# Undivided exponentials, value products with queries on partitions, and head pairs transposed on TensorE in a hybrid attention layer

## The chip, the cores and the metric

The kernel runs on one core of one Trainium2 chip. The metric is the device time of one execution in microseconds (us), lower is better. A core has five engines that run their own instruction streams in order: TensorE (PE, matrix products; PEld are its weight loads), VectorE (DVE), ScalarE (ACT), GpSimd (POOL) and SyncE (SP), which here issues all the transfers. Engines wait for one another by semaphores. Everything is computed in float32, with products split into a high and a low part of lower precision.

## The reference, cut to what matters

One encoder layer on x of 1024 tokens by 1024 channels. Eight latent heads attend to all earlier chunks of 64 tokens; eight chunked heads attend to a band of nine chunks with a position bias. The heads' outputs are laid side by side and multiplied by w_out; a gated MLP follows, which the change does not touch.

```python
def mla_attention(q, k, v):          # per block of 128 queries
    s = einsum('bqhd,bkhd->bhqk', qi, k) * scale
    s = where(mask, s, NEG_INF)
    p = softmax(s, axis=-1)
    return einsum('bhqk,bkhd->bqhd', p, v)

def chunk_attention(q, k, v, rel_bias):   # per chunk of 64 queries, 576 keys
    s = einsum('bqhd,bkhd->bhqk', qch, kb) * scale + bias
    s = where(valid, s, NEG_INF)
    p = softmax(s, axis=-1)
    return einsum('bhqk,bkhd->bqhd', p, vb)
...
mixed = dot(concatenate([o_mla, o_ca], -1), w_out)
x = x + g_a * mixed
```

Both heads have a value width of 64. The mask of the latent heads, in tiles of 128 queries, gives query tile i the keys of tiles 0 to i; a chunked head's tile i takes tiles i-4 to i.

## The kernel before, in words

The program is built by Tile: the Python code traces instructions, pools of named buffers ("tags", each with a number of bufs) give them memory, and a scheduler puts them in an order per engine by priorities and by a timeline of its own, so the order on an engine is not that of the code. A new tile of a tag waits until a buffer of that tag is free.

Attention is cut into units of four query tiles of one head (class Unit). `units` lists first the chunked units c{pair}{odd}, by pair of heads, half g of the sequence and odd or even head, then the latent units m{group}{head}, each head with g = 0 and g = 1 one behind the other. For each tile, `scores` (L634) makes the products q·k in PSUM (tag S, two buffers), the row minimum on DVE (L667 to L675), the exponential on ACT with the sum of the row in rsum (L681), the reciprocal of the sum on DVE (L683, L684), and then, in pieces of at most 640 keys, the divided exponentials as a half-precision high part on POOL (`scale_pool`, L71 from L698) and the rest as a low part on DVE (L701). Both parts lie in one tile of tag HL (three buffers), which a transposing DMA turns into tile PT (L703, three buffers). Exponentials of up to 640 keys lie in tag P (three buffers), longer ones in tag pg (six buffers), which also holds pages of the projections.

`values` (L707) runs three tiles behind `scores` (DEPTH). It multiplies the values with the transposed parts: the stationary operand is the stack of V's high and low part (64 + 64 columns), the moving one the 128 queries, so PSUM tile pv (one buffer, four query tiles side by side) has the head's channels on partitions, V's high part on one half and its low part on the other. After the fourth tile ACT scales one half into sb (L721), DVE adds the other (L722), and the 64 by 512 result goes to DRAM tile oT_d (L723), which holds all heads with channels on partitions.

`qk_page` (L612) makes the pages of q and k of a unit: four transposes on PE into PSUM tag T (one buffer), then a high part on ACT and a low part on DVE, in SBUF tags Q (two) and K (three).

Fillers are products that `pace` draws between the tiles: projections f_v, f_qk, f_m, the latent up-projections f_up (many small operations on POOL), and last f_oca, the output projection of the chunked heads. f_oca (L596) reads oT_d per tile of 128 tokens into `cl`, splits it on ACT (`ch`, L75) and POOL (`cl`, L82), multiplies by w_out and keeps the result in part_d. f_ada loads pieces of w_ada in between. Behind the attention, the loop at L855 does the same for the latent heads (ol, oh), adds part_d, makes the gated residual and the second norm (xn), and transposes it for the MLP (ht_ps).

Row tiles (rtile, tag R, four buffers) and square tiles (qtile, tag sq, two) are of equal size.

Of the kernel before, what the change touches and what calls it, by code (L numbers as in the profile page):

```python
# [41 lines left out]
MODE_C = "1111"  # L42
MODE_M = "1111"
# [3 lines left out]
# columns of the packed constants  # L47
# [15 lines left out]
def layer_kernel(ctx, tc, I, out):  # L63
# [3 lines left out]
    def f32(ap):  # L67
        return ap.bitcast(F32)
# [17 lines left out]
    oT_d = dram.tile([ND, P, S], F32, name="oT_d")  # L86
# [3 lines left out]
    # ---------------- constants  # L90
# [53 lines left out]
    def gemm3(pt, pairs, start=True, stop=True):  # L144
        """pairs: (stationary_hi, stationary_lo, moving_hi, moving_lo)"""
        n = len(pairs)
        for i, (sh, sl, mh, ml) in enumerate(pairs):
            pe.matmul(pt, sh, mh, start=(start and i == 0), stop=False)  # L148
            pe.matmul(pt, sh, ml, start=False, stop=False)  # L149
            pe.matmul(pt, sl, mh, start=False, stop=(stop and i == n - 1))  # L150
# [16 lines left out]
    # ---- weights of one column block of the input projection, split once  # L167
# [23 lines left out]
    # ---- x: statistics and normalised rows  # L191
# [42 lines left out]
    for d in range(ND):  # L234
# [10 lines left out]
        # modT rows: 0 = gain of the norm * (1 + scale), 1 = shift  # L245
# [13 lines left out]
    # ---- rotary tables  # L259
    def rope_tables():  # L260
# [56 lines left out]
        # per token: [g1 cos | g2 cos | g1 sin | g2 sin]  # L317
# [13 lines left out]
    # ---- exact power-of-two scales that bring V into half precision's range, from a bound on |V|:  # L331
    # |sum_d x_d w_d|^2 <= n * sum_d b_d^2 w_d^2
# [83 lines left out]
    # ---- the other adaLN rows  # L416
# [32 lines left out]
    def gate_bcast(pt, acc, c0, w, alloc):  # L449
        """column sums of acc, and b_ada, on every partition"""  # L450
# [53 lines left out]
    # ---- q_up / kv_up of 4 heads: token-layout q, k (normalised, rotated) and V stacks  # L504
# [78 lines left out]
    # ---- output projection of the chunked heads, kept aside in DRAM  # L583
# [11 lines left out]

    def f_oca():  # L596
        for n in range(2):
            ws = load_wo(4, n, "a", "p")
            for t in range(NT):
                lo = rtile(f"cl{t}_{n}", (P, 4, P), F32R)  # L600
                hi = rtile(f"ch{t}_{n}", (P, 4, P), F32R)
                sp.dma_start(f32(lo[:]), oT_d[4:8, :, t * P:(t + 1) * P].rearrange("k p t -> p k t"))
                hi_of("a", hi[:], f32(lo[:]))
                lo_of("p", lo[:], f32(lo[:]), hi[:])
                pt = ps.tile([P, 512], F32, name=f"oc{t}_{n}", tag="mm", bufs=2)
                yield from gemm3_f(pt[:], [(hi[:, k], lo[:, k], ws[k][:, 0], ws[k][:, 1]) for k in range(4)])
                o = qtile(f"co{t}_{n}")
                act.activation(o[:], pt[:], AF.Copy)
                sp.dma_start(part_d[t][:, n * 512:(n + 1) * 512], o[:])
# [16 lines left out]
    class Unit:  # L626
        """4 query tiles of one head"""

        def __init__(u, nm, base, rows, pages, vst, g, band, bias, odd, dst_d, vs):
            u.nm, u.base, u.rows, u.pages, u.vst, u.g = nm, base, rows, pages, vst, g  # L630
            u.band, u.bias, u.odd, u.dst_d, u.vs = band, bias, odd, dst_d, vs
            u.pt = {}

        def scores(u, i):  # L634
            """scores of one query tile and their softmax, transposed in two half-precision parts"""
# [5 lines left out]
            rsum = cst.tile([P, 1], F32, name=f"rs{nm}", tag="rsum", bufs=4)  # L641
            ri = cst.tile([P, 1], F32, name=f"ri{nm}", tag="ri", bufs=4)
            with tc.high_priority(offset=OFF_S):
# [37 lines left out]
                act.activation(pr[:, :n], sv, AF.Exp, bias=m[:], scale=-1.0, accum_out=rsum[:, 0:1])  # L681
            with tc.high_priority(offset=OFF_P):
                dve.reciprocal(ri[:], rsum[:, 0:1])  # L683
                dve.tensor_scalar(ri[:], ri[:], PSCALE, None, op0=MUL)  # L684
                u.pt[i] = []
                for x, (p0, p1) in enumerate(pieces):
# [3 lines left out]
                    cnt[0] += 1  # L690
                    mode = (MODE_C if u.band else MODE_M)[cnt[0] % 4]
                    if mode == "2":
                        scale_pool(pp, pp, ri[:])
                        act.activation(hl[:, :w], pp, AF.Copy)
# [342 lines left out]
```

## Time and profile before

| | us |
|---|---|
| median of three runs | 1521.95 (1520.9, 1521.95, 1524.99) |
| span of the profiled execution | 1526.0 |
| PE busy | 1338.1 (88%) |
| DVE busy | 824.4 (54%) |
| POOL busy | 664.7 (44%) |
| ACT busy | 487.4 (32%) |
| DMA queue of SP, share of 16 engines | 36.0% |
| mean granted clock of PE | 0.928 |

Busy time is an average over stages with different limits, so it is read stage by stage, by windows of the trace. A waiting instruction holds up what stands behind it on its engine. In rows of the trace, `out<-in` are names of tiles; "idle before" is the time that the engine waited ahead of the instruction and what released it. Names end in m for latent heads and in c for chunked ones (Pm, hlm, PTm, sm, pvm); L numbers are lines of the kernel before.

### The profile page before, as it was taken

The page shows a single profiled execution, that of the slowest core. Times are in us where ns is not written, and L with a number is a line of the kernel's source. Part 1 is how long each engine was busy: PE and PEld are TensorE (multiplying, and loading weights), DVE is VectorE, ACT ScalarE, POOL GpSimd, SP SyncE. Part 2 cuts the span into 40 slices and gives each one's busy share as a digit, 9 for nine tenths or more (in the row PEclk, how much of TensorE's full clock was granted, in tenths as well). Part 3 has the DMA queues.
Part 4 walks back from the last instruction along what each step waited for, and adds up shares of the span by engine and source line. Part 5 has one row for each costly group of instructions (what it writes and reads, how often), then busy time and mean ns, then how long its engine had stood idle before and what let it go on. Part 6 is the DMA issues. An engine that isn't in the chain of part 4 may idle for free.

```text
span 1526.0 us, 19445 instructions
## 1 busy us (share of the span) xinstructions
PE 1338.1 (88%) x7100; PEld 1111.0 (73%) x7100; DVE 824.4 (54%) x1536; ACT 487.4 (32%) x919; POOL 664.7 (44%) x720
## 2 busy tenths in 40 slices
PE   3859989998767888858739999999999999999997
PEld 2749878987646666646528888888888888888885
DVE  6864786566768768843742433344334343434343
ACT  5443353343545545532413211212122121221200
POOL 5264463473799735435725231514314142341510
PEclk9979978989878899977859999999999999999998
DMA  7323657463613678787142110202112020110202
GB/s 270 133 67 73 138 119 142 121 131 94 122 40 70 150 143 174 165 181 247 56 138 69 56 55 28 70 30 67 42 42 69 15 83 28 56 56 28 70 1 110
DMA packets 202460, 142.90 MB, mean 94 GB/s; under 512 B 146294, under 2 KB 181242, under 8 KB 201340
## 3 DMA queue, kind: packets, MB, share of 16 engines
q1 hardware_dynamic: 202364, 141.66, 36.0%
q8 instruction: 56, 0.92, 0.3%
q14 instruction: 40, 0.33, 0.1%
HBM read 93.90 MB, written 13.11 MB: 70 GB/s over the span
## 4 chain that ended last, share of the span: by engine, by line
PE 63%; DMA 14%; DVE 10%; POOL 7%; issue 3%; ACT 2%; SPq 1%; POOLq 0%; DVEq 0%; ACTq 0%
PE up L148 10%; PE up L149 10%; PE up L150 10%; DMA aw<-w_ada 6%; PE dn L148 5%; PE dn L149 5%; PE dn L150 5%; DMA PTm<-hlm 4%; PE sc L656 2%; DVE adacc L241 2%; DVE aacc L428 1%; PE sm L656 1%; PE pvc L714 1%; POOL hlm L71 1%; DMA adaw<-w_ada 1%
## 5 line engine op out<-in xcount | busy, mean ns | idle before, releaser
L148 PE MATMUL up<-hT,wu_h 128*128 128x512 f32 x704 | 275.1, 391 | 0.0
L149 PE MATMUL up<-hT,wu_h 128*128 128x512 f32 x704 | 274.3, 390 | 0.0
L150 PE MATMUL up<-hT,wu_l 128*128 128x512 f32 x704 | 274.1, 389 | 0.0
L951 DVE TENSOR_TENSOR x<-x,dn 128x1024 f32<-128x1024 f32 x88 | 107.4, 1220 | 179.8 <-PE dn L150 179.8
L924 DVE SCALAR_TENSOR_TENSOR u<-up,pk,u 128x1023 f32<-128x1023 f32 x44 | 56.4, 1283 | 232.1 <-ACT u L923 232.1
L923 ACT ACTIVATE u<-up,pk 128x1024 f32<-128x1024 f32 x44 | 53.1, 1208 | 386.0 <-PE up L150 386.0
L149 PEld LDWEIGHTS up<-hT,wu_h 128*128 128x128 f32 x704 | 132.4, 188 | 28.0 <-issue 0.5
L148 PEld LDWEIGHTS up<-hT,wu_h 128*128 128x128 f32 x704 | 132.4, 188 | 27.9 <-issue 0.5
L82 POOL TENSOR_TENSOR wu_l<-wu_r,wu_h 128x1024 fp32r<-128x1024 f32 x44 | 105.7, 2402 | 107.9 <-PE up L149 60.1
L150 PEld LDWEIGHTS up<-hT,wu_l 128*128 128x128 f32 x704 | 132.4, 188 | 27.7 <-POOL wu_l L82 0.2
L77 POOL TENSOR_SCALAR wd<-wd_r 128x1024 fp32r<-128x1024 f32 x22 | 23.1, 1050 | 290.2 <-PE dn L150 289.1
L148 PE MATMUL dn<-wd,g 128*128 128x512 f32 x352 | 138.0, 392 | 5.0 <-ACT g L75 5.0
L149 PE MATMUL dn<-wd,g 128*128 128x512 f32 x352 | 137.9, 392 | 0.0
L150 PE MATMUL dn<-wd,g 128*128 128x512 f32 x352 | 137.4, 391 | 0.0
L71 POOL TENSOR_SCALAR hlm<-Pm,rim 128x512 f16<-128x512 f32 (+4 forms) x88 | 62.8, 717 | 69.1 <-DMA PTm<-hlm 46.6
L75 ACT ACTIVATE wu_h<-wu_r 128x1024 fp32r<-128x1024 f32 x44 | 46.5, 1057 | 141.1 <-DMA wu_r<-w_up 141.1
L938 POOL TENSOR_TENSOR wd_r<-wd_r,gmbc 128x1024 f32<-128x1024 f32 x22 | 52.6, 2392 | 80.6 <-DMA wd_r<-w_down 80.6
L701 DVE SCALAR_TENSOR_TENSOR hlm<-Pm,rim,hlm 128x512 f16<-128x512 f32 (+4 forms) x88 | 70.2, 801 | 31.7 <-POOL hlm L71 31.4
L148 PEld LDWEIGHTS dn<-wd,g 128*128 128x128 f32 x352 | 66.6, 189 | 19.4 <-issue 5.4
L71 POOL TENSOR_SCALAR hlc<-Pc,ric 128x640 f16<-128x640 f32 (+2 forms) x64 | 45.9, 719 | 78.5 <-DVE ric L684 38.9
L656 PE MATMUL sm<-mk,mq 96*128 96x512 f32 (+3 forms) x288 | 70.0, 375 | 9.8 <-ACT Pm L681 9.0
L656 PE MATMUL sc<-k,q 64*128 64x512 f32 (+3 forms) x288 | 71.2, 376 | 7.4 <-ACT Pc L681 4.9
(276 smaller groups left out, 3031.8 us busy)
## 6 DMA issues: line engine op xcount, KB each, us to landing
wu_r<-w_up SPq DMA_DIRECT2D x44, 512.0 KB, 3.6
aw<-w_ada SPq DMA_DIRECT2D x96, 128.0 KB, 2.2
wd_r<-w_down SPq DMA_DIRECT2D x22, 512.0 KB, 3.5
x<-x SPq DMA_DIRECT2D x16, 512.0 KB, 9.3
adaw<-w_ada_a SPq DMA_DIRECT2D x8, 1024.0 KB, 4.8
wq_r<-w_qk SPq DMA_DIRECT2D x32, 128.0 KB, 2.6
wor<-w_out SPq DMA_DIRECT2D x16, 256.0 KB, 3.0
cl<-oT_d SPq DMA_DIRECT2D x16, 256.0 KB, 3.3
```

The costliest lines, as they stand in the source:

```text
L71: pool.tensor_scalar(o, i, s, 1.0, op0=MUL, op1=MUL)
L75: act.activation(o, i, AF.Copy)
L82: (pool if eng == "p" else dve).tensor_tensor(o, i, f32(hi), op=SUB)
L148: pe.matmul(pt, sh, mh, start=(start and i == 0), stop=False)
L149: pe.matmul(pt, sh, ml, start=False, stop=False)
L150: pe.matmul(pt, sl, mh, start=False, stop=(stop and i == n - 1))
L656: last = pe.matmul(s[:, c:c + w], qpg[rs_, a, q], kpgs[kh][rs_, b, ko:ko + w], start=(a == 0 and b == 0), stop=(a == 1))
L701: dve.scalar_tensor_tensor(hl[:, w:2 * w], pp, ri[:], hl[:, :w], op0=MUL, op1=SUB)
L923: act.activation(u[:], pt[:], AF.Identity, scale=pk[:, cv + 2:cv + 3], bias=pk[:, cv + 3:cv + 4])
L924: dve.scalar_tensor_tensor(u[:, 1:], pt[:, :S - 1], pk[:, cv + 1:cv + 2], u[:, 1:], op0=MUL, op1=ADD)
L938: pool.tensor_tensor(raw[:], raw[:], gmbc[:], op=MUL)
L951: dve.tensor_tensor(x1[t][:], x1[t][:], pt[:], op=ADD)
```

## The change

- Exponentials are split undivided: the high and low part are made with the constant PSCALE in place of PSCALE over the sum of the row. The sums of a unit's four tiles are kept in one tile of 128 by 4.
- The value product swaps its operands: the transposed exponentials are stationary, the stack of V moves, so that pv has queries on partitions and, for each query tile, 64 columns of V's high part and 64 of its low part.
- After four tiles, ACT copies one half, DVE adds the other, and POOL multiplies by the reciprocals of the sums. Both heads of a pair write into one tile of 128 queries by 4 tiles by 128 channels.
- After the odd head, qk_page transposes that tile on PE through PSUM tag T into a page of tag K, with high and low part made there, and the page (512 KB) goes to DRAM; oT_d is now a separate tile per pair and half.
- f_oca and the loop behind the attention load these pages instead of splitting on ACT and POOL. f_oca holds four pages of tag pg for a half of the sequence and all eight weight tiles of both column halves; its loops are exchanged.
- Tags R (four) and sq (two) become one tag R of five; tag sb goes, and tag o has three buffers for one; rsum and ri change from four buffers of one column to three of four columns.
- Modes that were not in use, and comments, are gone.

```diff
-    oT_d = dram.tile([ND, P, S], F32, name="oT_d")
+    oT_d = [[dram.tile([P, 2, 512], F32, name=f"oT_d{k}_{h}") for h in range(2)] for k in range(ND)]
...
-        return apg.tile(list(shape), dt, name=name, tag="R", bufs=4)
+        return apg.tile(list(shape), dt, name=name, tag="R", bufs=5)
...
-        return apg.tile([P, 512], F32, name=name, tag="sq", bufs=2)
+        return apg.tile([P, 512], F32, name=name, tag="R", bufs=5)
...
+    def load_oT(k, h, name):
+        pg = pgtile([P, 2, 512], F32R, name)
+        sp.dma_start(f32(pg[:]), oT_d[k][h][:])
+        return pg
+
     def f_oca():
-        for n in range(2):
-            ws = load_wo(4, n, "a", "p")
-            for t in range(NT):
-                lo = rtile(f"cl{t}_{n}", (P, 4, P), F32R)
-                hi = rtile(f"ch{t}_{n}", (P, 4, P), F32R)
-                sp.dma_start(f32(lo[:]), oT_d[4:8, :, t * P:(t + 1) * P].rearrange("k p t -> p k t"))
-                hi_of("a", hi[:], f32(lo[:]))
-                lo_of("p", lo[:], f32(lo[:]), hi[:])
...
+        ws = [load_wo(4, n, "a", "p") for n in range(2)]
+        for h in range(2):
+            pgs = [load_oT(4 + k, h, f"ocl{k}_{h}") for k in range(4)]
+            for j in range(4):
+                sl = slice(j * P, (j + 1) * P)
+                for n in range(2):
+                    pt = ps.tile([P, 512], F32, name=f"oc{h}{j}_{n}", tag="mm", bufs=2)
+                    yield from gemm3_f(pt[:], [(pgs[k][:, 0, sl], pgs[k][:, 1, sl], ws[n][k][:, 0], ws[n][k][:, 1])
+                                               for k in range(4)])
...
-                dve.reciprocal(ri[:], rsum[:, 0:1])
-                dve.tensor_scalar(ri[:], ri[:], PSCALE, None, op0=MUL)
...
-                            scale_pool(hl[:, :w], pp, ri[:])
-                        dve.scalar_tensor_tensor(hl[:, w:2 * w], pp, ri[:], hl[:, :w], op0=MUL, op1=SUB)
+                    scale_pool(hl[:, :w], pp, PSCALE)
+                    dve.scalar_tensor_tensor(hl[:, w:2 * w], pp, PSCALE, hl[:, :w], op0=MUL, op1=SUB)
...
-                    last = pe.matmul(u.pv[:, c], u.vst(j), mov, start=(x == 0), stop=(x == len(todo) - 1))
+                    last = pe.matmul(u.pv[:, c], p, u.vst(j), start=(x == 0), stop=(x == len(todo) - 1))
...
-                    act.activation(sb[r0], u.pv[r1], AF.Copy, scale=inv[r1])
-                    dve.scalar_tensor_tensor(dst[r0], u.pv[r0], inv[r0], sb[r0], op0=MUL, op1=ADD)
-                    sp.dma_start(u.dst_d[r0, u.g * 512:(u.g + 1) * 512], dst[r0])
+                    if not u.odd:
+                        opair[u.pair, u.g] = at.tile([P, 4, 2, 64], F32, name=f"o{u.nm}_{u.g}", tag="o", bufs=3)
+                    o = opair[u.pair, u.g]
+                    ri = cst.tile([P, 4], F32, name=f"ri{u.nm}_{u.g}", tag="ri", bufs=3)
+                    dve.reciprocal(ri[:], u.rsum[:])
+                    pv = u.pv[:].rearrange("p (t a b) -> p t a b", t=4, a=2)
+                    act.activation(o[:, :, u.odd], pv[:, :, 1], AF.Copy)
+                    dve.tensor_tensor(o[:, :, u.odd], o[:, :, u.odd], pv[:, :, 0], op=ADD)
+                    pool.tensor_tensor(o[:, :, u.odd], o[:, :, u.odd], ri[:].unsqueeze(2).to_broadcast([P, 4, 64]), op=MUL)
+            if i % 4 == 3 and u.odd:
+                pg = qk_page(lambda j: o[:, j].rearrange("p a b -> p (a b)"), f"oT{u.nm}_{u.g}", P, "K", 3, vscale[u.vs][1])
+                sp.dma_start(u.dst_d[u.g][:], f32(pg[:]))
...
     for t in range(NT):
-        lo = gb.tile([P, 4, P], F32R, name=f"ol{t}", tag="ol", bufs=3)
-        hi = gb.tile([P, 4, P], F32R, name=f"oh{t}", tag="oh", bufs=3)
-        sp.dma_start(f32(lo[:]), oT_d[0:4, :, t * P:(t + 1) * P].rearrange("k p t -> p k t"))
-        hi_of("a", hi[:], f32(lo[:]))
-        lo_of("p", lo[:], f32(lo[:]), hi[:])
+        if t % 4 == 0:
+            oTs = []
+            for k in range(4):
+                pg = gb.tile([P, 2, 512], F32R, name=f"ol{k}_{t}", tag="ol", bufs=4)
+                sp.dma_start(f32(pg[:]), oT_d[k][t // 4][:])
+                oTs.append(pg)
```

More of the change, by code (lines that the diff above doesn't have):

```diff
@@ L626, in layer_kernel, with __init__ @@
     class Unit:
-        def __init__(u, nm, base, rows, pages, vst, g, band, bias, odd, dst_d, vs):
+        def __init__(u, nm, base, rows, pages, vst, g, band, bias, odd, dst_d, vs, pair):
             u.nm, u.base, u.rows, u.pages, u.vst, u.g = nm, base, rows, pages, vst, g
-            u.band, u.bias, u.odd, u.dst_d, u.vs = band, bias, odd, dst_d, vs
+            u.band, u.bias, u.odd, u.dst_d, u.vs, u.pair = band, bias, odd, dst_d, vs, pair
             u.pt = {}
@@ L640, in scores @@
             nm = f"{u.nm}_{i}"
[L641 to L642 removed]
+            if i % 4 == 0:
+                u.rsum = cst.tile([P, 4], F32, name=f"rs{nm}", tag="rsum", bufs=3)
             with tc.high_priority(offset=OFF_S):
@@ L866, in layer_kernel @@
             gemm3(pt[:, n * 512:(n + 1) * 512],
-                  [(hi[:, k], lo[:, k], wo[n][k][:, 0], wo[n][k][:, 1]) for k in range(4)])
+                  [(oTs[k][:, 0, sl], oTs[k][:, 1, sl], wo[n][k][:, 0], wo[n][k][:, 1]) for k in range(4)])
         dve.tensor_tensor(pa[:], pa[:], pt[:], op=ADD)
```

35 lines of the change are left out of this document (9 added, 26 removed).

## The prediction

> **What bounds the kernel now.** First the busy time by stretch. The stretches are cut where the trace changes work: 97 is the first product of f_v, 517 comes just after the last POOL step of f_up (L580, 515.2 us), 682 after the last value product (L714, 681.0 us), 794 at the first product of the MLP.
>
> ```profile
> core 0: us, PE busy (x) PEld busy (x) DVE busy (x) ACT busy (x) POOL busy (x), PEclk, DMA share, GB/s
> 97.00:400.00 303.00, 284.70 (x1999) 250.28 (x2000) 191.89 (x568) 123.98 (x334) 147.66 (x224) 0.91 0.54 117
> 400.00:517.00 117.00, 86.01 (x468) 68.61 (x467) 90.51 (x235) 63.68 (x154) 109.21 (x195) 0.81 0.35 77
> 517.00:682.00 165.00, 130.33 (x917) 103.17 (x914) 117.97 (x277) 77.00 (x159) 76.96 (x89) 0.93 0.78 163
> 682.00:794.00 112.00, 65.92 (x261) 50.18 (x261) 60.73 (x59) 30.69 (x47) 55.01 (x46) 0.71 0.46 152
> 794.00:1526.00 732.00, 722.09 (x3169) 596.59 (x3167) 287.48 (x220) 144.09 (x133) 231.59 (x110) 0.99 0.17 52
> ```
>
> The MLP (732 us) is PE alone, and the change leaves it as it is. Chunked heads and projections (303 us) have PE busy 94%. Up-projections beside the first latent heads (117 us) have POOL busy 93%. The latent heads (165 us) are full nowhere: PE 79%, DMA 78%, DVE 71%. The output projection (112 us) has no engine above 59%: a chain of waits. For the latent heads, the waits:
>
> ```profile
> POOL hlm L71 <- DMA PTm<-hlm: 46.6, 27, 3.7
> ...
> PE pvm L714 <- DMA PTm<-hlm: 17.5, 17, 2.4
> ```
>
> A piece (up to 640 keys of one query tile) is written by POOL into one of three hl buffers, completed by DVE, and transposed by DMA; POOL waits for a free hl 27 times in 67 pieces. These 67 pieces take 165 us, 2.46 us each. One turn of an hl buffer, 0.69 (POOL) + 0.74 (DVE) + 1.24 (issue) + 3.3 (median landing), about 6.0 us, over three buffers would allow 2.0 us. The rest is DVE's order; its groups here:
>
> ```profile
> L701 DVE SCALAR_TENSOR_TENSOR hlm<-Pm,rim,hlm 128x512 f16<-128x512 f32 x31 | 28.1, 908 | 16.7 <-POOL hlm L71 16.6
> ...
> L722 DVE SCALAR_TENSOR_TENSOR om<-pvm,vabm,sbm 64x512 f32<-64x512 f32 x12 | 8.9, 738 | 2.9 <-ACT sbm L721 2.7
> ...
> L683 DVE RECIPROCAL rim<-rsm 128x1 f32<-128x1 f32 x46 | 7.0, 153 | 5.0 <-ACT Pm L681 4.8
> L684 DVE TENSOR_SCALAR rim<-rim 128x1 f32<-128x1 f32 x46 | 6.8, 148 | 0.7
> ```
>
> **The change, part by part.** *Chunked heads (97 to 400).* Seven of the eight pages of head pairs fall here, each four transposes. Nearest row, over the whole attention:
>
> ```profile
> L82 POOL TENSOR_TENSOR cl<-cl,ch 128x512 fp32r<-128x512 f32 x16 | 20.7, 1293 | 10.7 <-ACT ch L75 9.0 <-PE pvm L714 1.8
> ...
> L616 PE MATMUL k_ps<-ident,qn 128*128 128x128 f32 x32 | 5.1, 276 | 0.5 <-DVE q L620 0.5
> ```
>
> 5.1/32 = 0.16 us, so 28 cost 4.5 us on the engine that is 94% busy. Against it stand PE's waits here for transposed pieces (8.5 us) and for exponentials (4.9), which a shorter softmax shortens. Bounds +4.5 and -5; I take +3. The swapped value products keep count and shape (128x128, f16, 219 ns median), so nothing; swapped operands are not in the trace, and I allow 10% of their 0.06 us spacing (about 1056 of them, 6 us) either way, hidden on latent heads.
>
> *Up-projections (400 to 517).* In the built order of POOL, 21 pieces precede the last step of f_up before the change, 13 after it. The cause is in the code: oca's four pages take four of the six pg buffers, which the six latT pages had held and from which score tiles over 640 keys (P of tiles 5, 6, 7) also come. Eight pieces (384, 512, 640 keys, then 512, 256, 512, 384, 512) leave POOL: 0.58 + 5 rows of 0.5 to 0.76 + 1.03 and so on, 5.9 us. One cl (1.29) and one weight residue (1.4) leave; two multiplies of om enter. No row has these (128x256, f32, broadcast): between 0.47 (a 128x256 on DVE) and 1.06 (POOL's 128x512 broadcast L371), I take 0.74, POOL's 128x256 L82. POOL is the bound, so 117 becomes 117 - 5.9 - 1.3 - 1.4 + 1.5 = 110: **-7**.
>
> *Latent heads (517 to 682).* The eight pieces arrive here: 75 x 2.46 = 184.7, **+20**. DVE loses the reciprocal and scale of each tile (7.0 + 6.8 = 13.8) and L722 (8.9); it gains 13 reciprocals of 128x4 (0.15) and 13 adds of 128x256 (0.47, as L409), 8.1, and seven pages at 0.74 (k, L623), 5.2: -9.4. L701 at 512 keys means 908 ns here and is 0.75 in the timeline where POOL has no two-input operation: over all 67 pieces 12.7 us of stretch, beside 23 such operations (cl and weight residues), 0.55 us each. Fifteen cl leave (-8.3), 14 shorter om enter (+3.9): -4.4. Together -13.8 us of DVE; on the path, with DVE at 71%, between none and all: I take two thirds, **-9**.
>
> [...]
>
> *The new order of latent heads.* PSUM "T" has one buffer and K three; after every odd head the page of the pair now takes both in turn between the q and k pages of the heads that follow. That page waits for the pair's last value product, ACT, DVE, POOL, and four transposes. In PE's built order mk02_1, the second key page of head 2, stood before the values of tile 4 of head 1; now it stands behind the values of tile 3 of head 2 (same for m10_1; m12 a tile earlier). Tile 4's scores are queued behind it, so the softmax chain runs dry: from landing of tile 3 to landing of tile 4, 0.61 (eight value products) + 0.62 (transposes) + 0.68 (ACT L622) + 0.75 (DVE) + 1.3 (scores) + 0.91 (memset, minimum) + 0.78 (exponential) + 1.03 + 1.02 (hi, lo) + 3.3 = 11.0 us instead of 2.46, a loss of 8.5. Full buffers then catch up at 2.0 instead of 2.46 for about eight pieces, 3.7. Three heads: 3 x 4.8 = **+14**; bounds 0 (oca products and queued pieces cover it) and 26 (no catching up).
>
> ACT gives up sbm (0.68 x 32) and ch, oh (0.63 x 24) and gains a 128x256 copy (0.47 x 32) and a page (0.69 x 16), at 47% load: nothing. Transfers: 56 issues of oT, cl, ol leave, 32 of 512 KB enter, with 4 MB more written and 2 MB more read; such transfers land in 2.6 to 4.4 us, the old in 2.3 to 4.0. In the latent heads their SP issues cover it; without that cover oc is late once, by 3.6 us. On SP the last oT issue now stands ahead of x1_3 to x1_7 and of ol's second half: these wait for the last pair's ACT, DVE, POOL, PE, ACT, DVE (0.47 + 0.47 + 0.74 + 0.62 + 0.69 + 0.74 = 3.7 us behind the last value product), under the first four tiles' 96 products (0.23 each, 22 us).
>
> *Output projection (682 to 794).* PE's timeline:
>
> ```profile
> 705.01 0.39 PE L150 MATMUL op<-wo,ol 128*128 128x512 f32 x1
> 711.92 0.69 PE L219 MATMUL ht_ps<-ident,xn 128*128 128x128 f32 x2 [6.51 <-POOL xn L71]
> ...
> 715.88 0.80 PE L150 MATMUL op<-wo,ol 128*128 128x512 f32 x1 [0.71 <-POOL ol L82]
> ```
>
> POOL makes xn between residues of ol (1.28 each, eight), which go. Of the gap, 6.5; of the slow clock behind it, 21 products at 0.43 instead of 0.23, 4.2; on the chain ahead of the first product oh 0.64 and ol 1.28: -12.6. Given back: all four buffers of ol hold the first half, so the second half's pages load only behind tile 3's products, 4.4 us (512 KB, adaw): **-8**; bounds -13 and 0.
>
> Sum: +3 - 7 + 20 - 9 + 14 - 8 = +13. The profiled span is 1526.0, 4.05 above the median of the runs, 1521.95; so 1539 in a profile, **1535** as a median.
>
> **The rivals.** *Faster: DVE sets the latent heads.* Speaks for it: DVE is 85% busy from 560 to 640 us, and its order keeps POOL and ACT waiting (POOL for L675, ACT for L675, 17.5 us). The stretch then scales with DVE per piece, 118/67 = 1.76 less 17 us of relief (no multiply of om collides) over 75, 1.53: 165 x (75 x 1.53)/(67 x 1.76) = 161, -4. With the drains absorbed, -4 - 7 + 1 - 8 = -18: 1504. Decides if the drained time is filled by queued pieces. *Much slower: transfers set it.* DMA 78%, no relief, drains in full: +20 + 26 - 7 + 4 - 8 = +35: 1557. *No net change:* the drains are hidden and the relief is as summed: 1522; also what comes out if POOL starts no sooner because it waits for hl anyway (27 of 67) and the order costs little.
>
> **How the numbers follow.** Forecast 0.46, faster rival 0.29, much slower 0.12, no net change 0.13. The forecast's own range, with terms off by half, is 1522 to 1549. The range for 8 in 10 takes in the faster rival's centre and the slow one: 1504 to 1558. A measurement of this kernel (runs 1520.9 to 1525.0) can tell 0.3%, 4.6 us: faster 0.30, same 0.14, slower 0.56.
>
> **What would show it.** In the changed profile: the last step of f_up some 7 to 10 us earlier, with 13 pieces before it; a gap of more than 6 us between transposed pieces of tiles 3 and 4 in heads m02, m10, m12; DVE per piece lower, L701 near 0.75; POOL's waits for PTm fewer; the MLP's first product later by about 13 us though the output projection is shorter by 8; PE of the MLP unchanged at 732. I am wrong if the latent heads end earlier than 682, if the gaps are absent, or if the output projection is not shorter.

## The result, and the profile after

The changed kernel takes 1583.09 us (median of four executions, 1579.43 to 1588.49), the kernel before 1523.08 beside it: a ratio of 1.0397, 95% interval 1.0374 to 1.0421. It is slower, as forecast, but 48 us above the forecast of 1535 and 25 above the upper end of the range. The profiled execution spans 1586.7 us against 1526.0.

The busy time by stretch of the changed kernel, cut where its work changes:

```profile
core 0: us, PE busy (x) PEld busy (x) DVE busy (x) ACT busy (x) POOL busy (x), PEclk, DMA share, GB/s
97.00:407.00 310.00, 289.59 (x2033) 254.09 (x2034) 185.42 (x468) 121.78 (x338) 152.14 (x235) 0.91 0.51 120
407.00:519.00 112.00, 75.53 (x358) 59.59 (x356) 73.86 (x167) 54.92 (x132) 97.91 (x185) 0.77 0.30 78
519.00:735.00 216.00, 171.20 (x1055) 134.50 (x1052) 121.80 (x239) 81.83 (x178) 68.92 (x102) 0.82 0.61 138
735.00:839.00 104.00, 63.07 (x263) 48.76 (x264) 60.82 (x59) 24.00 (x36) 41.97 (x38) 0.75 0.50 182
839.00:1586.00 747.00, 737.80 (x3170) 595.40 (x3168) 283.68 (x220) 144.06 (x133) 232.50 (x110) 0.99 0.16 51
```

The third stretch, the latent heads, is 216 us long where it was 165; DMA share and granted clock fell there (0.78 to 0.61, 0.93 to 0.82), PE is busy for 79% of it in both kernels, and the shares of DVE, ACT and POOL fell: no engine is fuller, the stretch is longer by waits and by a slower clock. The last stretch, the MLP, has the same matmuls (3170 and 3169) and PE is busy in them 738 instead of 722 us.

Cut at single instructions (the first product of ku, the last step of f_up, the last value product, the first product of the MLP), the difference of 60.7 us divides so:

| Step | before | after | difference | predicted |
|---|---|---|---|---|
| start to first ku (chunked heads, projections) | 403.8 | 418.6 | +14.8 | +3 |
| to the last step of f_up (up-projections) | 111.4 | 100.6 | -10.8 | -7 |
| to the last value product (latent heads) | 165.8 | 214.5 | +48.7 | +25 |
| to the first MLP product (output projection) | 112.6 | 105.6 | -7.0 | -8 |
| MLP to the end | 732.4 | 747.4 | +15.0 | 0 |

Of the 47.7 us that the sum of the prediction missed, 23.7 lie in the latent heads, 15.0 in the MLP and 11.8 in the chunked heads; the other two steps came out 2.8 us shorter than forecast.

The waits of the latent heads after the change (engine, line, releaser: us in total, times, longest):

```profile
POOL hlm L69 <- ACT Pm L683: 62.6, 26, 7.3
...
POOL hlm L69 <- DMA PTm<-hlm: 36.0, 23, 3.9
POOL om L715 <- DVE om L714: 30.0, 7, 7.4
PEld L704 <- DMA PTm<-hlm: 23.7, 22, 3.7
...
PE pvm L704 <- DMA PTm<-hlm: 16.1, 10, 3.4
```

Before, POOL waited mostly for a free hl buffer (46.6 us for landings). Now its longest wait is for the exponentials: the buffers stand empty because scores come late. PE waits for transposed pieces both with its products (17.5 us before) and, as the pieces are its weights now, with its loads. DVE's own groups in the same stretch did become cheaper:

```profile
L691 DVE SCALAR_TENSOR_TENSOR hlm<-Pm,hlm 128x512 f16<-128x512 f32 x35 | 28.0, 800 | 19.6 <-POOL hlm L69 19.6
...
L714 DVE TENSOR_TENSOR om<-om,pvm 128x256 f32<-128x256 f32 x15 | 6.2, 414 | 8.2 <-ACT om L713 7.9
L711 DVE RECIPROCAL rim<-rsm 128x4 f32<-128x4 f32 x13 | 2.2, 169 | 0.6 <-ACT Pm L683 0.5
```

The transposes of the chunked pairs, and PE's first wait of more than 2.5 us after the output projection began:

```profile
L618 PE MATMUL oTc_ps<-ident,oc 128*128 128x128 f32 x32 | 6.6, 342 | 2.3 <-POOL oc L715 2.3
```

```profile
766.73 0.47 PE L146 MATMUL op<-wo,ol 128*128 128x512 f32 x1 [2.53 <-DMA ol<-oT_d]
```

Thirty-two transposes fill 6.6 us, 0.21 each. The wait of 6.5 us for xn is gone; one of 2.5 us for the second half's pages has come. That wait was not made by the residues of ol, though. In the kernel before, POOL made none of them between 694.7 and 714.5 us; ahead of xn it waited for DVE's pa, added x and made the norm:

```profile
704.47 3.26 POOL L870 TENSOR_TENSOR x<-x,pa 128x1024 f32<-128x1024 f32 x1 [9.75 <-DVE pa L869]
...
710.74 1.12 POOL L71 TENSOR_SCALAR xn<-x,r 128x1024 f32<-128x1024 f32 x1
...
714.55 3.74 POOL L82 TENSOR_TENSOR ol<-ol,oh 128x512 fp32r<-128x512 f32 x3
```

Now the latent heads one by one, from the last piece of one head to the last of the next (in the order of the transposes on SP): m02 to m13 took 33.7, 25.4, 23.7, 26.0, 24.8 and 24.4 us before, and 36.1, 24.4, 38.2, 25.7, 38.2 and 25.0 after. Of m10 to m13 only the even heads grew, by 13 to 15 us; m02 was long before, too. The windows of m02, m03, m10, m11 and m12:

```profile
542.00:578.00 36.00, 31.93 (x175) 24.98 (x176) 19.71 (x42) 12.59 (x30) 8.21 (x14) 0.76 0.44 99
578.00:602.00 24.00, 18.70 (x142) 14.35 (x142) 15.96 (x31) 9.18 (x19) 8.50 (x12) 0.93 0.81 192
602.00:640.00 38.00, 30.74 (x156) 23.29 (x156) 19.36 (x40) 13.20 (x29) 7.87 (x14) 0.72 0.48 113
640.00:666.00 26.00, 19.65 (x137) 15.52 (x134) 16.87 (x32) 9.14 (x20) 7.84 (x13) 0.89 0.64 113
666.00:704.00 38.00, 31.48 (x176) 25.60 (x177) 20.04 (x46) 14.44 (x34) 7.98 (x15) 0.78 0.53 114
```

Behind the five engines' busy times stand the granted clock, the DMA share and GB/s. The even heads have a clock of 0.72 to 0.78 and a DMA share near one half; the odd ones 0.89 to 0.93 and 0.64 to 0.81. The hole inside m02 on SP and on PE:

```profile
553.00 2.61 SPq L693 DMA_TRANSPOSE PTm<-hlm  x2
...
566.48 1.34 SPq L693 DMA_TRANSPOSE PTm<-hlm  x1
```

```profile
551.88 0.39 PE L147 MATMUL oc<-wo,ocl 128*128 128x512 f32 x1
...
557.46 1.05 PE L704 MATMUL pvm<-vt,PTm 128*128 128x128 f16 x8
558.31 1.06 PE L618 MATMUL mk_ps<-ident,kn 128*96 128x128 f32 x4
560.14 2.86 PE L658 MATMUL sm<-mk,mq 96*128 96x128 f32 x8 [0.77 <-ACT mk L624]
562.80 0.63 PE L146 MATMUL oc<-wo,ocl 128*128 128x512 f32 x1
```

The values of tile 3 (its piece is the second of the two issued from 553.0) stand ahead of the second key page mk02_1; its scores follow at 560.1, and the next transpose is issued at 566.5. From the issue of tile 3 to that of tile 4 it is 12.1 us in m02 and 12.9 in m10, as the prediction described; in m12 it is 6.4, and 8.8 more ahead of its tile 0. An oc product takes 0.63 us at the end of the hole, 0.39 ahead of it; the granted clock is 0.50 from 558 to 566 us.

### The profile page after: what moved, and what is told of

Same layout as the page of the kernel before. It is cut to its first block, busy times and chain, and to the rows that moved or that the text cites. A ratio compares the mean times of both kernels' runs of the same rounds, so it can differ in the third digit from the quotient of the medians.

```text
span 1586.7 us, 19278 instructions
## 1 busy us (share of the span) xinstructions
PE 1385.7 (87%) x7164; PEld 1133.9 (71%) x7164; DVE 801.7 (51%) x1328; ACT 474.9 (30%) x911; POOL 639.5 (40%) x728
## 4 chain that ended last, share of the span: by engine, by line
PE 65%; DMA 13%; DVE 9%; POOL 6%; issue 4%; ACT 2%; SPq 1%; POOLq 0%; DVEq 0%; ACTq 0%
PE up L148 10%; PE up L146 10%; PE up L147 10%; PE dn L146 5%; PE dn L147 5%; PE dn L148 5%; DMA aw<-w_ada 4%; DMA PTm<-hlm 4%; PE sc L658 2%; PE sm L658 2%; PE pvm L704 2%; DVE adacc L239 1%; DVE aacc L426 1%; PE ipq L146 1%; DMA adaw<-w_ada_a 1%
## 5 line engine op out<-in xcount | busy, mean ns | idle before, releaser
L146 PE MATMUL up<-hT,wu_h 128*128 128x512 f32 x704 | 278.4, 395 | 0.0
L148 PE MATMUL up<-hT,wu_l 128*128 128x512 f32 x704 | 277.6, 394 | 0.0
L147 PE MATMUL up<-hT,wu_h 128*128 128x512 f32 x704 | 277.5, 394 | 0.0
L147 PEld LDWEIGHTS up<-hT,wu_h 128*128 128x128 f32 x704 | 131.9, 187 | 32.6 <-issue 0.5
L69 POOL TENSOR_SCALAR hlm<-Pm 128x512 f16<-128x512 f32 (+4 forms) x88 | 52.7, 603 | 109.3 <-ACT Pm L683 62.6
L658 PE MATMUL sm<-mk,mq 96*128 96x512 f32 (+3 forms) x288 | 79.2, 409 | 15.6 <-ACT Pm L683 8.7
L704 PE MATMUL pvm<-vt,PTm 128*128 128x128 f16 x576 | 55.0, 250 | 33.6 <-DMA PTm<-hlm 24.7
L691 DVE SCALAR_TENSOR_TENSOR hlm<-Pm,hlm 128x512 f16<-128x512 f32 (+4 forms) x88 | 59.4, 681 | 39.7 <-POOL hlm L69 39.6
L704 PEld LDWEIGHTS <-PTm 128*128 128x128 f16 x576 | 41.9, 113 | 49.8 <-DMA PTm<-hlm 34.1
```

The source lines that it names most:

```text
L69: pool.tensor_scalar(o, i, s, 1.0, op0=MUL, op1=MUL)
L658: last = pe.matmul(s[:, c:c + w], qpg[rs_, a, q], kpgs[kh][rs_, b, ko:ko + w], start=(a == 0 and b == 0), stop=(a == 1))
L691: dve.scalar_tensor_tensor(hl[:, w:2 * w], pp, PSCALE, hl[:, :w], op0=MUL, op1=SUB)
L704: last = pe.matmul(u.pv[:, c], p, u.vst(j), start=(x == 0), stop=(x == len(todo) - 1))
```

## The experiments

Each gives the ratio to the kernel before on the same chip. "After" is 1.0397.

### Are the empty stretches the shared T and K buffers?

```diff
-        pt = ps.tile(..., name=f"{name}_ps", tag="T", bufs=TB)
+        pt = ps.tile(..., tag="mm" if own and OWN_T else "T", ...)     # own: page of a latent pair
+        if own and OWN_K:
+            pg = [rtile(f"{name}_{b}", (P, 512), F32R) for b in range(2)]
```

tk_own sets both, t_own OWN_T alone, k_own OWN_K alone.

> The page of a pair of latent heads no longer shares PSUM T (it takes one of the two mm banks) nor the three K buffers (it takes two buffers of R). In the built order mk10_1 then stands ahead of all values of head m03 again. Theory (the shared buffers tie the next head's key page to the last values of the pair before): the gaps between transposed pieces in m02, m10 and m12 (12.1, 12.9, and 8.8 + 6.4 us in the changed kernel) fall to 5 us or less each, these heads take about 25 us as the odd ones do instead of 36 to 38, and the kernel takes 1583 - 36 = about 1547. Rival (the gaps are lost POOL, DVE or transfer time that would have to be spent anyway): the gaps move, and the time stays above 1573.

> Only PSUM T is taken from the page of the pair (it uses mm); K is still shared. If T alone ties the heads: about 1547, as with both apart. If K alone ties them: 1583. If either one is enough to tie them: mk10_1 now stands in the middle of the last head's values, and between a third and two thirds of the 36 us come back, 1559 to 1571.

> Only the K buffer is taken from the page of the pair (it uses R); T is still shared. If T alone ties the heads: 1583 within 6 us. If K alone ties them: about 1547. The built order of pages and values is nearly that of the changed kernel, so I expect 1583 within 6 us.

| Kernel | median us | ratio, 95% interval | gaps in m02, m10, m12 (tile 3 to 4) | last value product |
|---|---|---|---|---|
| after | 1583.09 | 1.0397, 1.0374 to 1.0421 | 12.1, 12.9, 6.4 | 733.7 |
| tk_own | 1560.96 | 1.0221, 1.0198 to 1.0245 | 2.1, 1.4, 1.4 | 693.5 |
| t_own | 1566.47 | 1.0257, 1.0234 to 1.0280 | 9.2, 7.9, 7.4 | 704.7 |
| k_own | 1591.67 | 1.0426, 1.0402 to 1.0449 | 11.9, 10.0, 6.2 | 724.9 |

With both apart these gaps are gone and the last value product comes 40 us earlier. With T alone apart 29 of the 40 us come back, though gaps of 7 to 9 us remain; with K alone apart 9 come back and the time does not fall. The two buffers tie the heads, T first. Against the kernel before, m02 to m13 together grew by 29.4 us (from the last piece of m01 to that of m13 187.5 us, and 158.0 before), nearly all of it in m10 and m12. In tk_own they take 147.3 us: its odd heads, too, are 3 to 5 us shorter than in the change. The windows of m02, m03 and m10 in tk_own, to set beside those above, and POOL's first wait in its latent heads:

```profile
543.00:569.00 26.00, 22.78 (x166) 18.37 (x165) 17.44 (x36) 12.10 (x27) 8.44 (x14) 1.00 0.72 168
569.00:590.00 21.00, 16.25 (x136) 12.55 (x135) 17.16 (x35) 9.80 (x22) 7.70 (x13) 1.00 0.62 121
590.00:622.00 32.00, 28.75 (x172) 23.18 (x171) 19.58 (x40) 12.18 (x27) 8.12 (x13) 0.84 0.79 196
```

```profile
POOL hlm L69 <- DMA PTm<-hlm: 96.3, 52, 6.2
```

m02 takes 26 us at the full clock, and POOL waits for landings again: the heads are fed. m10 still takes 32, at 0.84, with a gap of 7.2 us ahead of its tile 5. The time fell by 27 us of these 40 (0.0176 x 1523) because the output projection lost 13 (118.8 us from the last value product to the MLP, 105.6 in the change): its first product stands 15.3 us behind the last value product, 5.3 in the changed kernel. I put that down to my pages, which hold buffers of R through which the weights wo load; k_own, with the same pages, has 17.2 us there, and t_own, without them, 8.1.

### Is the MLP slower for its addresses?

```diff
+    cst.tile([P, 16], F32, name="pad")                    # pad64, in the changed kernel
...
+    lpool.__enter__().tile([P, n // 4], F32, name="lpad")  # b_lpad64, b_lpad32: kernel before, under x1 and hT
```

> The changed kernel with 64 unused bytes per partition among the constants. The change made the constants 64 bytes smaller, so x1 and the MLP's input pages hT stand 64 bytes lower than before, and everything else of the MLP where it stood. Theory (the place of hT costs the MLP's matmuls 4 ns each): the up-projection's matmuls go from a mean of 394 back to 390 ns, the MLP from 748 to 732 us, the kernel to 1583 - 15 = about 1568. Rival (the MLP is slower from something else, such as the clock after a longer attention): 394 ns and 1583 stay.

> The kernel before with 64 unused bytes under x1 and hT, which are laid out after the attention; nothing else moves. hT then stands 32 bytes above a multiple of 128, as in the changed kernel, instead of 96. Theory (the place of hT modulo 128 costs the up-projection's matmuls 4 to 5 ns): mean 394 ns instead of 390, MLP 747 instead of 732 us, 1524 + 15 = about 1539. Rival (only that one address of the changed kernel, or something else that its padding moved): 1524 within 4 us.

> The same with 32 bytes: hT stands on a multiple of 512. If what counts is hT's distance to the weights wu (96 above a multiple of 128, as hT before): slower than before by up to 15 us. If a row that begins on a multiple of 64 is read in fewer pieces: faster than before, by 0 to 15 us. No theory of mine tells which; 1524 within 3 us would say that only 32 above a multiple of 128 is bad.

pad64 took 1575.40 us, ratio 1.0322 (1.0294 to 1.0349): 11 us less than the change (0.0075 x 1523), where 15 were expected. In its profile the attention is as in the changed kernel (last value product 735.7) and the MLP takes 731.5 us instead of 747.4. The first products of the MLP (ns minimum, median, maximum, first and last start), before, after, pad64 and b_lpad32:

```profile
L148 PE MATMUL up<-hT,wu_h x704: 389/389/1415, 793.6 to 1491.0; 128*128 128x512 f32 x176
```

```profile
L146 PE MATMUL up<-hT,wu_h x704: 393/394/1303, 839.3 to 1551.4; 128*128 128x512 f32 x176
```

```profile
L147 PE MATMUL up<-hT,wu_h x704: 388/390/1416, 840.4 to 1537.2; 128*128 128x512 f32 x176
```

```profile
L148 PE MATMUL up<-hT,wu_h x704: 392/396/1415, 795.5 to 1509.7; 128*128 128x512 f32 x176
```

The minimum moves, not only the median, so it is each matmul and no wait. The second products of the MLP (dn), which do not read hT, have a minimum of 387 to 389 ns in all four. In all profiles of the study the MLP took 730.6 to 732.8 us where the first hT page stood at byte 53728 (twelve kernels), 746.9 to 748.4 at 53664 (six). In the kernel before, with nothing else moved, byte 53792 (b_lpad64: 1534.96 us, ratio 1.0043, 1.0023 to 1.0063) gave 739.8, and 53760 (b_lpad32: 1541.59, 1.0114, 1.0095 to 1.0133) 749.4. So the place of x1 and hT alone does it. The rule that I expected (32 above a multiple of 128 is bad) fell: a multiple of 512 is as bad, and 53792 lies between. Nor was a start on a multiple of 64 (53760) faster. Which places are good, beyond these four, stays open.

### What made the chunked heads late: POOL's multiply, or the five common buffers?

```diff
-  pool.tensor_tensor(o[:, :, u.odd], o[:, :, u.odd], ri[:]..., op=MUL)
+  dve.tensor_tensor(o[:, :, u.odd], o[:, :, u.odd], ri[:]..., op=MUL)    # a_dve
...
-  rtile: tag="R", bufs=5    qtile: tag="R", bufs=5     o: bufs=3
+  rtile: tag="R", bufs=4    qtile: tag="sq", bufs=2    o: bufs=2         # a_r42
```

b_r5 puts rtile and qtile into five common buffers in the kernel before.

> The changed kernel with only the multiply of the outputs by the inverse sums moved from POOL to DVE. If the costs add up: 1583 - 12 = 1571 (first ku product 4 us earlier than 418.6, f_up's end earlier by as much). If they hide one another (the drains of m02, m10 and m12 set the latent heads, and the multiply is one link of the page's chain): the start is earlier but the gaps stay near 12 us, 1575 to 1580.

> The changed kernel with the raw rows in four buffers and the squares in two of their own, as before the change (the change put both into five common ones); the outputs o have two buffers instead of three to pay for it. Theory (the shared buffers made the projections late, as they did alone in the kernel before: first ku 403.8 to 413.4, first piece of m00 440.4 to 451.0): first ku product near 409 instead of 418.6, first piece of m00 near 446 instead of 456, and 1583 - 10 = about 1573. Rival (the transposes and the T buffer make them late): within 4 us of 1583.

> The kernel before with the squares (qtile) and the raw rows (rtile) in five common buffers, as in the change, instead of two and four. In the built order 17 pieces stand ahead of the last step of f_up instead of 21. If the shared buffers hold back the projections: first ku product later than 403.8 by 3 us or more, and 1523 + 5 to 10. If not: 1523 within 3 us.

| Kernel | median us | ratio, 95% interval | first ku | last value product |
|---|---|---|---|---|
| before | 1523.08 | 1 | 403.8 | 681.0 |
| after | 1583.09 | 1.0397, 1.0374 to 1.0421 | 418.6 | 733.7 |
| a_dve | 1570.20 | 1.0308, 1.0283 to 1.0334 | 405.7 | 711.1 |
| a_r42 | 1580.49 | 1.0355, 1.0332 to 1.0378 | 409.3 | 722.6 |
| b_r5 | 1540.96 | 1.0121, 1.0090 to 1.0151 | 413.4 | 683.3 |

Moving 16 multiplies of 0.62 us in the chunked heads brings ku forward by 12.9 us. Their length, 11.5 us in all, does not explain that by itself, as POOL is busy for only 152 of the 310 us of this stretch. The wait in the changed kernel's chunked heads, and POOL's instructions around one of them:

```profile
POOL oc L715 <- DVE oc L714: 27.8, 11, 7.8
```

```profile
360.65 0.22 POOL L466 TENSOR_TENSOR kr<-lat 128x16 f32<-128x16 f32 x1
368.68 0.79 POOL L715 TENSOR_TENSOR oc<-oc,ric 128x256 f32<-128x256 f32 x1 [7.81 <-DVE oc L714]
370.68 0.30 POOL L484 TENSOR_SCALAR mss<-mss 128x1 f32<-128x1 f32 x1 [1.21 <-ACT msq L481]
```

POOL stands still for 7.81 us until the pair's last value product, ACT's copy and DVE's add are done; behind it in POOL's order come the norms of the latent projection, and nothing of POOL starts in these 7.81 us.

That this wait is what made ku late is not shown. Here the norm behind the multiply waited another 1.21 us for ACT's msq, so the multiply held up nothing directly. In eight of the eleven places the next instruction of POOL waited on for an input or a buffer of its own; the waits in the other three are 5.8 us together (0.36, 3.58, 1.89). And a_dve is not the changed kernel with one operation moved: the scheduler laid out the rest anew, on POOL from the second chunked unit on, so the queue and the new order are not told apart. The profiles also vary: four kernels with one and the same order on PE (before, b_swap, b_lpad64, b_lpad32) have their first ku at 400.4 to 405.2 us.

The time fell by 13.6 us (0.0089 x 1523), near the 12.9 gained at ku: the cost of the multiply adds to that of the gaps, which stayed (11.8, 12.8, 7.0), and does not hide behind them. (The profiled execution of a_dve is the quickest of its four and that of the change the slowest of its own, so their last value products differ by more; 9.7 of these 22.6 us lie behind ku.)

The common buffers cost the kernel before 18 us: ku is 9.6 us later, and at the end the oca products run on to 702.4 us, 19 behind the last value product (in the kernel before they end 20 ahead of it). In the changed kernel taking them apart brings ku forward by 9.3 us but only 6 us of time, against the 10 expected; its output projection took 9 us more (114.6). The two repairs, 12.9 and 9.3 us alone, are more than the 14.8 us that there were to gain, so they overlap.

### Do the eight pieces cost where they lie?

```diff
-            pgs = [load_oT(4 + k, h, f"ocl{k}_{h}") for k in range(4)]
             for j in range(4):
+                pg = pgtile([P, 4, 2, P], F32R, f"ocl{h}{j}")
+                for k in range(4):
+                    sp.dma_start(f32(pg[:, k]), oT_d[4 + k][h][:, :, sl])
```

tks_pad is tk_own with this and the padding; all_pad parts the page from T and K in the chunked heads too.

> tk_own, and f_oca loads its pages in slices of 128 queries, one pg buffer a slice instead of four at once, with the 64 bytes of padding. In the built order 23 pieces stand ahead of the last step of f_up (13 in the changed kernel, 21 before it). Theory (P of m00's tiles 5 to 7 waits for pg buffers that ocl took): the gap between pieces of tiles 4 and 5 of m00, 16.2 us, goes to under 5, m00 ends by 495 instead of 517 us, the last value product comes some 20 us earlier, the padding gives 15: 1561 - 35 = about 1526. Rival (POOL sets the up-projections, so each piece that comes back lengthens them by as much): f_up ends ten pieces of 0.6 us later, and the gain beside the padding is 5 us or less: 1541 to 1546.

> tks_pad with the page of the pair apart (mm and R) in the chunked heads too. Theory (the shared T and K cost the chunked heads their 7 us as well): last chunked value product at 412 instead of 418.5 us and 5 to 7 us less than tks_pad. Rival (the 7 us are the transposes on a busy PE and the five shared R buffers): within 3 us of tks_pad, or slower, as the page now takes R too.

tks_pad: 1539.20 us, 1.0099 (1.0063 to 1.0135). The pieces move as said (m00 ends at 496.6 instead of 517.2 in tk_own), but the last step of f_up comes at 531.1 instead of 521.1 and the last value product at 691.7 instead of 693.5. From ku to the last step of f_up it takes 12.3 us more than in tk_own, and the latent heads 11.8 less: ten pieces moved and 1.8 us gained. That is what the rival said, POOL does them in either place. all_pad: 1548.81 us, 1.0166 (1.0117 to 1.0216), ipq ends 11 us later than in tks_pad (323.0 against 311.6), presumably as R is short in the projections. It tells nothing for or against T in the chunked heads.

### The parts alone in the kernel before

```diff
-                dve.reciprocal(ri[:], rsum[:, 0:1])
-                dve.tensor_scalar(ri[:], ri[:], PSCALE, None, op0=MUL)     # b_und
...
-                    last = pe.matmul(u.pv[:, c], u.vst(j), mov, ...)
+                    last = pe.matmul(u.pv[:, c], mov, u.vst(j), ...)       # b_swap
...
+                    act.activation(hi[r0], dst[r0], AF.Copy)
+                    dve.tensor_tensor(dst[r0].bitcast(F32R), dst[r0], f32(hi[r0]), op=SUB)   # b_pages
```

> The kernel before with undivided exponentials and nothing else; the division by the sums is left out altogether, so the output is not the reference's. It takes two small DVE operations off every tile (0.30 us each time) and their wait out of the chain from exponential to hi. Theory (DVE sets the latent heads in part): heads m03 to m13 take 22 to 23 us instead of 24.4 to 26, and 1523 - 12 = about 1511. Rival (transfers or POOL set them): heads unchanged within 0.5 us, 1523 within 4 us.

> The kernel before with the operands of the value products swapped and nothing else; what follows takes them as if they were not, so the output is not the reference's. The order on PE is that of the kernel before, instruction by instruction. The prediction's term: nothing, 1523 within 6 us. Rival (the transposed piece is now loaded as weights, 64 us of stalled loads in the changed kernel, where V could be loaded ahead of it): the value products' loads wait, and 1529 or more.

> The kernel before with the change's output projection alone: the outputs of the heads are stored in two parts (hi by ACT, lo by DVE, each half a pair, no transposes), ocl is loaded in slices, ol in pages. Theory (the 8 us of the output projection come from the residues that leave POOL there, and need nothing of the new attention): 682 to 794 becomes 104 us, POOL loses 8 cl beside the latent heads, the attention stays within 4 us: 1523 - 8 = about 1515. Rival (the second part and its store hold the single buffers sb and o longer and delay the values): attention later by 8 us or more, 1523 or above.

b_swap: 1526.16 us, 1.0001 (0.9985 to 1.0018): swapped operands cost nothing. b_und: 1530.26 us, 1.0042 (1.0022 to 1.0062): the two small operations a tile gave nothing. Its last five heads take 124.4 us together, and those of the kernel before 124.4. POOL now waits for landings 38 times where it was 27:

```profile
POOL hlm L71 <- DMA PTm<-hlm: 50.4, 38, 4.1
```

b_pages: 1540.98 us, 1.0110 (1.0077 to 1.0142), against an expected 1515. From the last value product to the first MLP product it is 115.4 us, and 112.6 before: the output projection as the change writes it isn't shorter by itself. No residue of ol stands on POOL there, and PE's wait for the first xn is longer than the 6.51 us of the kernel before:

```profile
728.60 0.69 PE L219 MATMUL ht_ps<-ident,xn 128*128 128x128 f32 x2 [10.11 <-POOL xn L71]
```

The kernels that keep the changed output projection and end their attention in other ways gave 114.6 (a_r42), 115.0 (tks_pad), 118.8 (tk_own), 106.6 (a_dve) and 105.6 (the change).

### Can the parts be put together?

tks_dve is tks_pad with the multiply on DVE; tks_dve_wor also loads the last weights wo through pg. best1 holds the page of a pair in pg instead of R, with a_r42's buffers, the slices and the padding; best1_dve adds the multiply on DVE.

> All repairs together: the page of a pair of latent heads in mm and in a pg buffer, ocl in slices, raw rows and squares apart with two buffers of o, and 64 bytes of padding. By the runs so far: 1539 of the kernel with the page in R, less 10 for the buffers of the projections, less up to 10 because the weights wo (which go through the squares' buffers) load ahead of the end of the attention again: 1519 to 1529. If it is 1535 or more, the repairs do not add up, and something else of the change sets the latent heads.

> tks_pad (page in mm and R, ocl in slices, 64 bytes) with the multiply of the output by the inverse sums on DVE instead of POOL (0.62 us on POOL, 32 times). Theory (POOL sets the up-projections and delays the residues of the projections, so its 20 us of multiplies are part of the 16 us left): first ku product 3 us or more earlier than 417.3, f_up's last step 4 us or more earlier than 531, and 1539 - 8 = about 1531. Rival (the chain of the page is as long on DVE, and POOL's work there waits for landings anyway): 1539 within 4 us.

> tks_dve (1526.9), and the last eight weight slices wo load through pg buffers instead of R, which the pages hold at the end. In the built order two of the eight loads stand ahead of the last four transposes. Theory (the first product of the output projection stands 12.5 us behind the last value product for wo's sake, 5.8 before the change): the distance falls to 6 to 8 us and the kernel to 1527 - 5 = about 1522, 4 us less than the kernel before. Rival (ol and the rest of wo still load behind the last transposed piece): 1525 to 1528.

> The page in a pg buffer, raw rows and squares apart, two buffers of o, ocl in slices, 64 bytes, and the multiply on DVE. With POOL's multiply this one took 1543 and tks_pad 1539, so I expect 1543 - 12 = about 1531; below 1523 it would be the best version.

| Kernel | median us | ratio, 95% interval |
|---|---|---|
| best1 | 1543.01 | 1.0116, 1.0097 to 1.0136 |
| tks_dve | 1526.86 | 1.0006, 0.9996 to 1.0016 |
| tks_dve_wor | 1525.43 | 1.0004, 0.9987 to 1.0022 |
| best1_dve | 1548.26 | 1.0158, 1.0139 to 1.0177 |

Step by step the ratio goes from 1.0397 (the change) to 1.0221 (T and K apart), 1.0099 (padding and slices) and 1.0006 (the multiply on DVE): 27, 19 and 14 us. tks_dve takes back the whole loss: ku at 412.6, f_up's end at 516.5, last value product at 677.9 (681.0 before), MLP 732.7. What it is ahead there it loses to wo (12.5 us from the last value product to the first of the output projection, 5.8 before). tks_dve_wor cut that to 9.2 us, not to 6 to 8, and is no faster than the kernel before that can be told. best1_dve took 17 us more than expected; its m01 takes 48.4 us (32.6 in tks_dve_wor), 21.7 of them ahead of the first piece of tile 7. Its code differs from best1's by the multiply alone, and it is 6 us slower (0.0042 x 1523), so moving the multiply gained 14 us twice and lost 6 once. Why the same repairs with other buffers don't add up I have not settled: the scheduler orders each variant anew, and this one was not taken apart.

## Why the prediction was right or wrong

**Direction and place.** "Slower", through the order of the latent heads, was right, and its test held: the gaps of more than 6 us stand in m02, m10 and m12 and go when T and K are parted. The likeliest case's time and the range were not: the new order, the chunked heads and the MLP were priced too low, and the relief of DVE and the output projection had the wrong reasons. The rival nearest in time, "much slower" at 1557, is not borne out either: it had transfers as the bound, and the DMA share of the latent heads fell from 0.78 to 0.61. Of what was to show it, the 13 pieces, fewer waits for PTm (23 for 27), L691 near 0.75 (0.80) and the shorter output projection came; f_up's end came 4 us later instead of 7 to 10 earlier, the MLP's first product 46 us later instead of 13, and PE's time in the MLP did not stay.

**The new order, +14 (bounds 0 and 26).** Mis-sized: m02 to m13 grew by 29.4 us, and tk_own gives 40 us of attention back. The single gap was near the working in two of three heads (12.1 and 12.9 from issue to issue, 6.4 in m12; 11.0 worked out). Wrong was "full buffers then catch up": an even head takes 36 to 38 us against 24 to 26 of an odd one, so nothing is caught up. In the hole PE runs at half the clock (0.50 from 558 to 566 us, 0.72 to 0.78 over the head), scores take longer (a 96x512 product means 628 ns there, and 403 from 587 to 591 us at a clock of 1.00), and the first tile of the even head waits too (5.6, 4.4 and 8.8 us), which I had not counted. My upper bound was therefore no bound.

**Chunked heads, +3.** It was +14.8. I costed the transposes and left out two things. The multiply of om got a duration, but its place in POOL's order, where it waits for 27.8 us in 11 waits, no price. And I did not weigh that squares and raw rows went from two and four buffers to five in common. a_dve brings ku to 405.7 and a_r42 to 409.3, from 418.6. By which instructions the multiply's place makes ku late stays open.

**Up-projections, -7.** -10.8, with the 13 pieces ahead of the last step that the built order showed. But the term was of little worth: tks_pad moved pieces back and gained 1.8 us. There the up-projections grew by 12.3 us and the latent heads shrank by 11.8, where I had booked 7 and 20.

**DVE relief, -9.** Its largest part is not there: without the reciprocal and the scale of each tile (13.8 us of DVE) b_und left 124.4 us at 124.4. That speaks against the rival that DVE sets the latent heads, and against the working's "the rest is DVE's order". The other parts of the relief were not tested alone. With both buffers parted, tk_own needs 172.4 us for 75 pieces, 2.30 each against 2.47 before, so +20 - 9 came to +6.6; what took the 0.17 I did not separate.

**Swapped products, nothing.** Right: 1.0001.

**Output projection, -8.** -7.0 measured, by luck and not for my reason. I put the gap of 6.5 us down to residues that leave POOL; in the trace of before none of them stands ahead of that xn, b_pages without them waits 10.11 us for it and needs 2.8 us more than before, and the same code in a_r42 needs 9.0 more than in the change. The pages of ol took 6.6 us to land (median), where I had put 4.4. What sets this span stays open. That it depends on when wo and the pages have landed, and that the change's starved latent heads gave the loads time, was not tested by itself.

**MLP, "leaves it as it is".** +15.0, a quarter of the loss. The change made the constants 64 bytes smaller, and with them put back pad64 has the MLP at 731.5 us. No row of the profile of before could have told it; a comparison of the two address maps would have shown that hT moved.

**DVE beside POOL.** Part of the -9 was an estimate from the timeline of before: 0.55 us of stretch of L701 for each operation of POOL with two inputs. Of 30 rows of L701 with 128x512 in the latent heads there, 23 had no such operation beside them (21 took 0.66 to 0.75 us, two 1.27 and 1.28), and the seven beside one took 0.73 to 1.77. No run shows by itself that the one lengthens the other. In the trace of the change, 20 of the 32 multiplies take 0.61 to 0.62 us and 12 take 0.66 to 1.20; each of these 12 began while a two-input operation of DVE ran, as three of the 20 did. But it is 3.8 us in all, too little for the 13.6 of a_dve. The 512-key residues on DVE took a mean of 800 ns after and 908 before in the latent heads, with several causes at once.

## What to carry to other kernels

For every buffer that a change joins, ask who takes turns with it: here two shared buffers, T and K, cost about 27 us. For every instruction that it puts on an engine's queue, ask what it waits for there, and try it on another engine: 32 multiplies of 0.62 us, moved from POOL to DVE, gained 14 us in two kernels and lost 6 in a third, so such a repair holds for the kernel in which it was measured. Work that moves to the next stage can cost there what it saved here: ten pieces moved, 1.8 us gained. Before believing that an untouched stage stays as it was, compare where its tiles lie.

## What the runs showed of the hardware

The place of a matmul's operand in SBUF told in this MLP. With x1 and hT 64 bytes lower, the 128x512 products that read hT went from a median of 389 to 394 ns (minimum 389 to 393) at a granted clock of 0.99 in both, and the MLP took 15 us more; with the 64 bytes put back (pad64) it was 390 (minimum 388). In the kernel before, with nothing else moved, 32 bytes higher gave 396 (minimum 392).

The granted clock fell to half without a long stop. Around the hole of m02, from 550 to 566 us, the longest single wait of PE was 1.70 us, and the granted clock was 0.98 from 550 to 554 us and 0.50 from 558 to 566; an oc product went from 0.39 to 0.63 us. What made the clock fall no run shows by itself.
